# q, k and v as seven-for-eight block products, and linear attention by token tiles

## The chip, the cores and the metric

The kernel runs on one core of one Trainium2 chip. The time is device microseconds of that core for one execution of the whole program; of several executions the median is given.

## The reference

One decoder layer over 1024 tokens of 1024 features: a gated linear attention (GLA) mixer and a squared-ReLU MLP, each behind an RMS norm and with a residual, then a last RMS norm.

```python
h = rms_norm(x, norm_mix)
q, k, v, r, gk_low = split(h @ w_in, [512, 1024, 2048, 3072])      # 4 heads, 128 for q and k, 256 for v and r
log_a = log_sigmoid(gk_low @ w_gk_up + b_gk) / 16                  # one decay for each token and feature of k
# for each head, in chunks: b = cumsum(log_a) inside the chunk
o     = (q * exp(b)) @ state + causal(sum_c q_c k_c exp(b_i - b_j)) @ v
state = state * exp(b_last) + (k * exp(b_last - b)).T @ v
x = x + (rms_norm(o, g_onorm) * silu(r)) @ w_out
x = x + square(relu(rms_norm(x, norm_ffn) @ w_ff1)) @ w_ff2
out = rms_norm(x, final_norm)
```

All in float32. w_ff1 is 1024 x 4096.

## The kernel before

**Products.** `mm3` makes one product of 128 rows by 128 by up to 512 columns as three matmuls: `split` (L84 to L87) cuts each operand into a high part (a rounding copy on ACT, L86) and a low part (the difference, on DVE, L87), and PE adds hi x hi, hi x lo and lo x hi in PSUM. PSUM has eight banks, five of the tag `gl` and three of `mm`.

**The mixer.** A loop over the eight 128-row slices of x (`load_x`) makes q, k and v of head 0. The split x stays in SBUF, in eight tiles `big` (X(half, high or low, slice)), for the whole mixer. Then the heads follow one another. `gate` (L308) makes the decay of a head and half of the tokens: one matmul, Abs, Exp, Ln and Relu on ACT, an add and four scans on DVE. `prep_fast` (L329) scales q and k by the exponentials, `scores_fast` makes the scores of four token tiles as plain fp32 products and splits what the rest needs. `chunk` (L410) does one token tile of one head: new state (three passes of 256 columns), output from scores and v (three passes), output from q and the state (three passes, both split), and the row norm. `chunk_out` (L457) transposes the output into `og`. PE's order is written out by hand: `head_steps` lists the steps of each head, and between them stand pieces of `fill`, the plain projections of q, k, v and r of the later heads (`q_steps`, `v_steps`, `r_steps`, eight slices each, v with 256 columns and q, k, r with 512). DMAs of weights come by `unit` on SP's queue, one tile `raw` of 512 KB each, and are split when they land.

**Block products.** From L597 on, w_out and the MLP are done with 2 x 2 blocks and seven products for eight (`form`, `Side`, `step`, `plan`): each step is 48 matmuls of 512 columns (four lanes of 128 rows, four slices, three passes), needs a new pair of split operands (four `big` tiles, sums on DVE or POOL first), and the lanes' banks go by a sink to their place. `operand` issues the operands of the next step ahead of the current one; ACT's, DVE's and SP's order is set by the scheduler from that.

Of the kernel before, what the change touches and what calls it, by code (L numbers as in the profile page):

```python
# [48 lines left out]
def hybrid_trunk(ctx: ExitStack, tc: tile.TileContext, x, xT, w_head, w_r, w_gk, w_up,  # L49
# [6 lines left out]
    BUFS = dict(big=8, raw=2, w8=3, v8=2, qk=5, og=8, L=2, t4=3, at=1, t2=1, c4=2,  # L56
                S=1, Shl=1, on=2, wup=1, st=8, mm=3, gl=5)
    SHAPE = dict(big=[P, 4, 512], raw=[P, 1024], w8=[P, 2, 1024], v8=[P, 2, 1024], qk=[P, 1024],
                 og=[P, 1024], L=[P, 2, 512], t4=[P, 2, 512], at=[P, 512], t2=[P, 2, 512],
                 c4=[P, 1024], S=[P, DV], Shl=[P, 2, DV], on=[P, DV], wup=[P, 512], st=[P, 8],  # L60
                 mm=[P, 512], gl=[P, 512])
    count = [0]

    def new(tag, dtype=F32):
        count[0] += 1
        pool_ = ps if tag in ("mm", "gl") else sb
        return pool_.tile(SHAPE[tag], dtype, tag=tag, bufs=BUFS[tag], name=f"{tag}{count[0]}")

    def f32(ap):
        return ap.bitcast(F32)  # L70

    def flat(ap):
        return ap.rearrange("p a b -> p (a b)")
# [49 lines left out]
    dma = {}  # L123

    def unit(src, tag="w8"):

        raw = new("raw")
        hl = [new(tag, F32R), new(tag, F32R)] if tag == "c4" else new(tag, F32R)
        hi, lo = hl if tag == "c4" else (hl[:, 0, :], hl[:, 1, :])
        with tc.high_priority():  # L130
            dma["unit"] = nc.sync.dma_start(raw, src)
            split(hi, lo, raw)
        return hi, lo

    def run(general):
        stat = {n: sb.tile([P, w], F32, tag=n, bufs=1, name=f"{n}{int(general)}")
                for n, w in dict(ss1=8, rstd1=8, ss2=8, rstd2=8, rstd3=8).items()}
        ss1, rstd1, ss2, rstd2, rstd3 = (stat[n] for n in ("ss1", "rstd1", "ss2", "rstd2", "rstd3"))

        xs = [[[new("big", F32R) for kh in range(2)] for hl in range(2)] for hf in range(2)]

        def X(hf, hl, kt):
            return xs[hf][hl][kt // 4][:, kt % 4, :]

        def xtok(t, hl, kt):
            return X(t // 4, hl, kt)[:, (t % 4) * P:(t % 4) * P + P]

        xraw = {}  # L150

        def scaled_x(kt, hf, raw):
            r, g = raw[:, hf * 512:(hf + 1) * 512], g_mix[:, kt:kt + 1]
            dve.tensor_scalar(X(hf, 0, kt), r, g, None, op0=ALU.mult)
            dve.scalar_tensor_tensor(X(hf, 1, kt), r, g, f32(X(hf, 0, kt)), op0=ALU.mult, op1=ALU.subtract)  # L155

        def load_x(kt):
            raw = new("og")
            order_after(tc, nc.sync.dma_start(raw, xT[kt * P:(kt + 1) * P, :]), dma["unit"], wait=False)
            for hf in range(2):  # L160
                scaled_x(kt, hf, raw)

        def first():

            xr, wr = new("og"), new("raw")
            w = new("w8", F32R)
            hi, lo = w[:, 0, :], w[:, 1, :]
            with tc.high_priority():
                nc.sync.dma_start(xr[:, 0:512], xT[0:P, 0:512])
                nc.sync.dma_start(wr[:, 0:512], w_head[0, 0][:, 0:512])  # L170
                nc.sync.dma_start(xr[:, 512:], xT[0:P, 512:])
                dma["unit"] = nc.sync.dma_start(wr[:, 512:], w_head[0, 0][:, 512:])
                for cs in (slice(0, 256), slice(256, 512)):
                    split(hi[:, cs], lo[:, cs], wr[:, cs])
                scaled_x(0, 0, xr)
                scaled_x(0, 1, xr)
                split(hi[:, 512:], lo[:, 512:], wr[:, 512:])
            return hi, lo

        pq = [new("mm") for _ in range(2)]  # L180
        pk = [new("mm"), new("gl")]
        pv = [new("gl") for _ in range(4)]
        rbc = new("c4")

        def qk_part(kt, w, hf, passes=(0, 1, 2)):
            for o, c0 in ((pq, 0), (pk, P)):
                for n in passes:
                    mm(o[hf], w[n // 2][:, c0:c0 + P], X(hf, n % 2, kt), kt == 0 and n == 0, kt == KT - 1 and n == 2)

        def v_part(kt, w, hf, passes=(0, 1, 2)):  # L190
            for t in range(4 * hf, 4 * hf + 4):
                o = pv[t // 2][:, (t % 2) * DV:(t % 2) * DV + DV]

                for n in passes:
                    mm(o, xtok(t, n % 2, kt), w[n // 2][:, 256:512],
                       kt == 0 and t % 2 == 0 and n == 0, kt == KT - 1 and t % 2 == 1 and n == 2)

        def token_rms():
            for t in range(TT):
                xr = new("og")  # L200
                nc.sync.dma_start(xr, x[t * P:(t + 1) * P, :])
                act.activation(xr, xr, AF.Square, accum_out=ss1[:, t:t + 1])
            rstd_of(rstd1, ss1, 8, D)

        def spread_rms():
            dg = new("t2")
            for hf in range(2):
# [36 lines left out]
        def half(hf):  # L244
            return slice(hf * 512, hf * 512 + 512)
# [741 lines left out]
```

## Time and profile before

| | |
|---|---|
| time, three runs | median 1040.15 us (1038.79 to 1040.63) |
| the profiled execution | 1039.07 us, its span 1037.4 us |
| PE, busy | 1024.9 us |
| DVE, busy | 706.0 us |
| ACT, busy | 535.2 us |
| SBUF and HBM traffic by DMA | 127.65 MB, 123 GB/s in the mean |
| w_out's first product starts | 334.47 us |

The span is cut into 40 equal slices in the page, and the digit of a slice is its busy share in tenths. A row of the order in time reads: start, length, engine, line, operation, written tile <- read tiles, shapes, count. A group reads: line, engine, operation, tiles, shape, count | busy us, mean ns | idle before, and what ended it. As matmuls overlap, the time of one is best read from the start of a row to the start of the next.

### The profile page before, as it was taken

The page shows a single profiled execution, that of the slowest core. Times are in us where ns is not written, and L with a number is a line of the kernel's source. Part 1 is how long each engine was busy: PE and PEld are TensorE (multiplying, and loading weights), DVE is VectorE, ACT ScalarE, POOL GpSimd, SP SyncE. Part 2 cuts the span into 40 slices and gives each one's busy share as a digit, 9 for nine tenths or more (in the row PEclk, how much of TensorE's full clock was granted, in tenths as well). Part 3 has the DMA queues.
Part 4 walks back from the last instruction along what each step waited for, and adds up shares of the span by engine and source line. Part 5 has one row for each costly group of instructions (what it writes and reads, how often), then busy time and mean ns, then how long its engine had stood idle before and what let it go on. Part 6 is the DMA issues. An engine that isn't in the chain of part 4 may idle for free.

```text
span 1037.4 us, 13340 instructions
## 1 busy us (share of the span) xinstructions
PE 1024.9 (99%) x5122; PEld 871.8 (84%) x5122; DVE 706.0 (68%) x976; ACT 535.2 (52%) x922; POOL 187.5 (18%) x135
## 2 busy tenths in 40 slices
PE   8999999999999999999999999999999999999996
PEld 8989999889888888888888888888888888888885
DVE  7565746467657998879977327976337975438975
ACT  2545747467666357766532447332437331547355
POOL 0000101000000000022404430404430304431261
PEclk9999999999999999999999999999999999999998
DMA  8501111111303433575132674043664044662004
GB/s 282 218 26 37 41 41 42 42 31 52 101 2 133 152 87 116 202 265 211 33 103 101 243 284 163 1 122 105 269 234 162 2 121 161 246 233 90 1 1 166
DMA packets 61977, 127.65 MB, mean 123 GB/s; under 512 B 3920, under 2 KB 36816, under 8 KB 54736
## 3 DMA queue, kind: packets, MB, share of 16 engines
q1 hardware_dynamic: 61760, 126.70, 34.6%
q8 instruction: 42, 0.69, 0.3%
q14 instruction: 31, 0.25, 0.1%
q10 hardware_dynamic: 144, 0.01, 0.0%
HBM read 107.82 MB, written 18.87 MB: 122 GB/s over the span
## 4 chain that ended last, share of the span: by engine, by line
PE 97%; DVE 1%; ACT 1%; DMA 1%; issue 1%; SPq 0%; ACTq 0%; DVEq 0%
PE gl L77 51%; PE mm L77 44%; PE mm L775 1%; PE gl L461 1%; DMA og<-in_xT 1%; PE gl L363 0%; ACT st L845 0%; ACT og L850 0%; DVE big L155 0%; DVE st L848 0%; DVE t L729 0%; DVE w L87 0%; ACT st L846 0%; ACT og L844 0%; DVE qk L729 0%
## 5 line engine op out<-in xcount | busy, mean ns | idle before, releaser
L77 PE MATMUL gl<-big,big 128*128 128x512 f32 x2052 | 476.2, 390 | 0.0
L77 PEld LDWEIGHTS gl<-big,big 128*128 128x128 f32 x2052 | 384.7, 188 | 79.2
L77 PE MATMUL mm<-big,big 128*128 128x512 f32 x972 | 228.9, 389 | 0.0
L77 PEld LDWEIGHTS mm<-big,big 128*128 128x128 f32 x972 | 182.5, 188 | 37.8
L87 DVE TENSOR_TENSOR big<-w,big 128x1024 fp32r<-128x1024 f32 x90 | 128.5, 1457 | 98.3 <-ACT big L86 98.3
L77 PE MATMUL mm<-big,w 128*128 128x512 f32 x744 | 180.5, 393 | 1.5 <-ACT w L86 1.0
L77 PEld LDWEIGHTS mm<-big,w 128*128 128x128 f32 x744 | 136.4, 188 | 28.1 <-ACT w L86 1.2
L86 ACT ACTIVATE big<-w 128x1024 fp32r<-128x1024 f32 x90 | 91.3, 1052 | 117.5 <-PE gl L77 55.0
L624 POOL TENSOR_TENSOR w<-w,w 128x1024 f32<-128x1024 f32 x28 | 77.9, 2796 | 159.6 <-DVE big L87 159.3
L624 POOL TENSOR_TENSOR w<-w,v 128x1024 f32<-128x1024 f32 x14 | 33.3, 2398 | 327.7 <-DVE big L87 327.1
L87 DVE TENSOR_TENSOR big<-og,big 128x1024 fp32r<-128x1024 f32 (+1 forms) x52 | 60.7, 1174 | 43.6 <-ACT big L86 43.6
L87 DVE TENSOR_TENSOR big<-v,big 128x1024 fp32r<-128x1024 f32 x36 | 49.0, 1376 | 37.9 <-ACT big L86 37.9
L86 ACT ACTIVATE big<-og 128x1024 fp32r<-128x1024 f32 (+1 forms) x52 | 47.0, 952 | 53.0 <-PE gl L77 32.5
L77 PE MATMUL mm<-w,big 128*128 128x256 f32 x576 | 73.0, 284 | 0.0
L77 PEld LDWEIGHTS mm<-w,big 128*128 128x128 f32 x576 | 70.9, 192 | 0.2
L86 ACT ACTIVATE big<-raw 128x1024 fp32r<-128x1024 f32 (+1 forms) x42 | 38.2, 935 | 61.1 <-DVE raw L624 33.7
L86 ACT ACTIVATE big<-v 128x1024 fp32r<-128x1024 f32 x36 | 36.6, 1048 | 54.4 <-PE mm L77 27.8
L87 DVE TENSOR_TENSOR big<-raw,big 128x1024 fp32r<-128x1024 f32 (+1 forms) x42 | 60.1, 1457 | 2.0 <-ACT big L86 2.0
L624 POOL TENSOR_TENSOR w<-v,w 128x1024 f32<-128x1024 f32 x14 | 41.1, 2945 | 44.7 <-DVE big L87 44.7
L86 ACT ACTIVATE w<-raw 128x1024 fp32r<-128x1024 f32 (+2 forms) x26 | 25.7, 992 | 39.8 <-PE mm L77 27.5
L798 ACT ACTIVATE og<-og 128x1024 f32<-128x1024 f32 x24 | 25.4, 1057 | 30.5 <-DVE og L791 30.5
L87 DVE TENSOR_TENSOR w<-raw,w 128x1024 fp32r<-128x1024 f32 (+2 forms) x26 | 29.6, 1141 | 15.6 <-ACT w L86 15.4
(209 smaller groups left out, 1010.7 us busy)
## 6 DMA issues: line engine op xcount, KB each, us to landing
big<-xv SPq DMA_DIRECT2D x42, 1024.0 KB, 6.9
xv<-big SPq DMA_DIRECT2D x14, 1024.0 KB, 4.9
v<-in_w_ff SPq DMA_DIRECT2D x32, 256.0 KB, 4.2
w<-in_w_ff SPq DMA_DIRECT2D x32, 256.0 KB, 4.3
w<-in_w_ff SPq DMA_DIRECT2D x16, 512.0 KB, 8.5
v<-in_w_ff SPq DMA_DIRECT2D x16, 512.0 KB, 6.6
raw<-in_w_head SPq DMA_DIRECT2D x15, 512.0 KB, 4.2
og<-in_x SPq DMA_DIRECT2D x8, 512.0 KB, 8.8
```

What stands on the lines that cost most here:

```text
L77: pe.matmul(o, w, m, start=start, stop=stop, skip_group_check=partial)
L86: act.activation(hi, src, AF.Copy)
L87: dve.tensor_tensor(lo, src, f32(hi), op=ALU.subtract)
L461: pe.transpose(tp[:, j * P:(j + 1) * P], on[:, j * P:(j + 1) * P], ident)
L624: self.eng.tensor_tensor(*(self.ap(b, kp, self.span) for b in (o, x_, y_)), op=op)
L775: pe.transpose(p_[:, c * P:(c + 1) * P], xn[4 * hf + c][:, kt * P:(kt + 1) * P], ident)
L798: act.activation(d2, d2, AF.Relu)
```

## The change

The block products now also serve the projections of the mixer. Plan (0) makes q and k of all heads at once: the weights of q and k (2 x 2 blocks of 512) are one side, x the other, seven steps. Plan (1) makes v the same way, with x as its stationary side. The x operands of plan (0) are written to DRAM (`keep`, `xv`) and read back for v and for r; those of steps 0 and 5 of plan (1) are made anew (`KeptX`). Plan (0) has three hooks: the first half of the gate's low-rank product after its first step (`gk_first`), the squares of x's rows (`token_rms`) and a split of block 12 (`x12_split`) ahead of its third step, and the second half (`gk_second`) ahead of its sixth. The gate and the scaling of q and k hang in plan (1) as hooks, as do the loads of r's weights and the first scores. The row scale of RMS norm is no longer applied to q, k and r as they leave PSUM but folded into the vectors `r_sq`, `r_qs`, `r_neg` and `r_ss`.

Then a loop goes over the eight token tiles, each step for all heads: new state, output, transposes of the tile before, and between them the four parts of r of the next tile, now with the tokens as the stationary side and 512 columns of w_r. The product of q with the state is one plain fp32 matmul of 256 columns instead of three passes, and its operands aren't split. w_out and the MLP keep their arithmetic; their tiles have other tags.

```diff
-        fill = (q_steps(1) + v_steps(1) + q_steps(2) + v_steps(2) + q_steps(3) + r_steps(0) + v_steps(3)
-                + r_steps(1) + r_steps(2))
...
+            for i, (_, _, _, sink, order) in enumerate(plan):
+                for at, n in enumerate(order):
+                    for f in hooks.get((i, at), ()):
+                        f()
+                    cur = ops.pop(0)
...
+                    if nxt[0] < len(plan):
+                        ops.append(operand(*nxt))
...
+        def qk_into(n, lane, p_):
+            d = qk_view(int(PART[n][0]) - 1, lane)[:, half(int(PART[n][1]) - 1)]
+            with tc.high_priority():
+                if n in (3, 4, 5):
+                    dve.tensor_tensor(d, p_, d, op=ALU.add)
+                else:
+                    act.activation(d, p_, AF.Copy)
...
+        def token_rms():
+            for t in range(TT):
+                xr = new("g4")
+                nc.sync.dma_start(xr, x[t * P:(t + 1) * P, :])
+                act.activation(xr, xr, AF.Square, accum_out=ss1[:, t:t + 1])
...
+            def split(self, n):
+                out = [kl(new("big", F32R)) for _ in range(2)]
+                for kh in range(2):
+                    if n in (0, 5):
+                        raw = new("raw")
...
+                        for k in range(2):
+                            scaled_split(out[kh][:, k, 0, :], out[kh][:, k, 1, :], raw[:, half(k)], kt + k)
+                    else:
+                        nc.sync.dma_start(out[kh].rearrange("p k l t -> p (k l t)").bitcast(F32), xv[n][kh])
...
+        def outputs(c):
...
+            for h in range(H):
+                d = o[h // 2][:, (h % 2) * DV:(h % 2) * DV + DV]
+                mm3(d, *hl_of(ah, h, P), *hl_of(v[c][h // 2], h % 2, DV), True, c == 0)
+                if c:
+                    mm(d, qk_view(0, h)[:, c * P:c * P + P], S[:, h * DV:h * DV + DV], False, True)
...
+        def load_wr(a, kq):
+            raw = new("raw")
+            for k in range(2):
+                nc.sync.dma_start(raw[:, half(k)].rearrange("p (f c) -> p f c", c=P),
+                                  w_r[4 * a:4 * a + 4, :, (2 * kq + k) * P:(2 * kq + k + 1) * P].rearrange("f p c -> p f c"))
+            w = kl(new("big", F32R))
+            split(w[:, :, 0, :], w[:, :, 1, :], raw.rearrange("p (k f) -> p k f", k=2))
+            wr[a, kq] = w
...
+        def r_part(t, n):
...
+            a, i = ((0, 0), (1, 0), (1, 1), (0, 1))[n]
...
+            for k in range(4):
+                kt = 4 * i + k
+                w = wr[a, kt // 2][:, kt % 2]
+                mm3(rbank[a], u[:, 2 * k, :], u[:, 2 * k + 1, :], w[:, 0, :], w[:, 1, :], kt == 0, kt == 7)
...
+        hooks = {(0, 1): (gk_first,), (0, 2): (token_rms, x12_split), (0, 5): (gk_second,)}
+        if not general:
+            hooks.update({(1, 0, 0, 3): (spread_rms,),
+                          (1, 0, 2, 3): (g(prep_fast, 0, 0, "mm"), g(prep_fast, 1, 0, "mm")),
+                          (1, 0, 3, 3): (g(prep_fast, 2, 0, "mm"),),
+                          (1, 1, 0, 1): (g(prep_fast, 3, 0, "mm"),),
+                          (1, 5, 2, 3): (g(prep_fast, 0, 1, "mm"),),
+                          (1, 6): tuple(g(load_wr, 0, kq) for kq in range(4)),
+                          (1, 6, 3, 1): (g(operands, 0, "mm"),)})
+        chunks_of([(wqk, xq, 0, qk_into, PLAIN), (KeptX(), wv, 1, v_into, PLAIN)], ops_a, hooks, {})
...
+        load_xt(0, 0)
+        load_xt(0, 1)
+        for kq in range(4):
+            load_wr(1, kq)
+        v_split(0)
+        for n in range(4):
+            r_part(0, n)
+        for c in range(TT):
...
+            more = c + 1 < TT
+            if more:
+                load_xt(c + 1, 0)
+                load_xt(c + 1, 1)
+                new_state(c)
+                r_part(c + 1, 0)
+            outputs(c)
+            if more:
+                v_split(c + 1)
+                r_part(c + 1, 1)
+                if not general:
+                    if c + 1 < H:
+                        prep_fast(c + 1, 1, "gl")
+                    operands(c + 1)
+                r_part(c + 1, 2)
+            if c:
+                outputs_T(c - 1, "gl")
+            if more:
+                r_part(c + 1, 3)
```

What moves on the engines, at three places. On PE, before: one tile of head 1's attention with the v product of head 2 behind it (on and L are the output and the scaled q or k, og 840 and 841 hold v's two parts, t the split scores, q and k, Shl the state, w the split v weights, big the x).

```order
L461 MATMUL gl_1550<-ident,on_1390 128x128 x2
L77 MATMUL gl_1556<-og_840,t_1433 128x256
L77 MATMUL gl_1556<-og_841,t_1433 128x256
L77 MATMUL gl_1556<-og_840,t_1433 128x256
L77 MATMUL gl_1555<-og_840,t_1431 128x256
L77 MATMUL gl_1555<-og_841,t_1431 128x256
L77 MATMUL gl_1555<-og_840,t_1431 128x256
L77 MATMUL gl_1555<-Shl_1493,t_1432 128x256 x3
L77 MATMUL mm_1583<-w_1513,big_88 128x256 x2
L77 MATMUL mm_1583<-w_1513,big_90 128x256
```

On PE, now: the second token tile (wa holds the split scores and k, wb v and the tokens of r, g_1599 the state in fp32, hq_291 and hq_300 q, big the r weights).

```order
L70 MATMUL gl_1745<-wb_1649,wa_1689 128x256 x6
L70 MATMUL gl_1746<-wb_1650,wa_1689 128x256 x6
L70 MATMUL mm_1769<-big_1391,wb_1739 128x512 x6
L70 MATMUL mm_1769<-big_1397,wb_1739 128x512 x6
L70 MATMUL gl_1784<-wb_1649,wa_1688 128x256 x3
L70 MATMUL gl_1784<-g_1599,hq_291 128x256
...
L70 MATMUL mm_1822<-big_1491,wb_1739 128x512 x6
L70 MATMUL mm_1822<-big_1497,wb_1739 128x512 x6
```

The state's update and the output of one head, three passes each, have become those of four heads in a row, with one fp32 matmul for the state's share, and what stands between is r at 512 columns instead of v at 256.

On ACT, before: the beginning of head 0's attention, where v of head 1 leaves PSUM (L262) and one weight unit is split (L86).

```order
L86 ACTIVATE w_1239<-raw_1238 128x1024
L453 ACTIVATE on_820,st_819<-gl_802 128x256
L442 ACTIVATE Shl_811<-S_809,st_807 128x256
L110 ACTIVATE st_819<-st_819,vec 128x1
L111 ACTIVATE st_819<-st_819 128x1
L455 ACTIVATE on_820<-gl_802,st_819 128x256
L262 ACTIVATE og_840<-mm_842,rstd_84 128x256
```

On ACT, now: from plan (0) to plan (1). The gl banks are those of the last q/k step, big_771 and big_772 x for v's first step (scaled by g_mix), big_787 and big_790 v's weights.

```order
L426 ACTIVATE hq_505<-gl_248 128x512
L426 ACTIVATE hq_505<-gl_252 128x512
L426 ACTIVATE hq_520<-gl_256 128x512
L426 ACTIVATE hq_520<-gl_260 128x512
L324 ACTIVATE big_771<-raw_773,vec 128x512 x2
L324 ACTIVATE big_772<-raw_779,vec 128x512 x2
L79 ACTIVATE big_787<-wa_679 128x2x512
L79 ACTIVATE big_790<-wa_680 128x2x512
L441 ACTIVATE vx_884<-gl_871,tok_88 128x512
```

Where one weight unit of 1024 stood ahead of the products that use it, there are now four evacuations of 512 columns and then the operands of the next step.

On DVE, before: the gate and scaling of head 0 (t_654 is the gate's input, qk_639 the decay, L_664 and L_674 the scaled q and k) with one weight unit between.

```order
L320 TENSOR_TENSOR t_654<-t_654 128x512
L342 TENSOR_TENSOR L_664<-L_664,qk_547 128x512
L324 SCALAR_TENSOR_TENSOR qk_639<-ones,t_654 128x128 x4
L251 SCALAR_TENSOR_TENSOR qk_625<-mm_697,c_104 128x512
L87 TENSOR_TENSOR w_836<-raw_835,w_836 128x1024
L333 TENSOR_TENSOR L_674<-qk_639 128x512
```

On DVE, now: the first steps of v. g_967 and g_1002 are the gates of heads 1 and 2, hq the q and k, vx the v tiles being added up, and big_1024 a weight operand of v's third step.

```order
L502 SCALAR_TENSOR_TENSOR g_967<-ones,g_967 128x128 x4
L516 TENSOR_TENSOR hq_505<-g_947,hq_505 128x512
L511 TENSOR_TENSOR g_967<-g_967 128x512
L515 TENSOR_TENSOR hq_291<-g_947,hq_291 128x512
L439 SCALAR_TENSOR_TENSOR vx_943<-mm_1082,tok_88,vx_943 128x512
L499 TENSOR_TENSOR g_1002<-g_1002 128x512
L516 TENSOR_TENSOR hq_505<-g_967,hq_505 128x512
L502 SCALAR_TENSOR_TENSOR g_1002<-ones,g_1002 128x128
L515 TENSOR_TENSOR hq_291<-g_967,hq_291 128x512
L439 SCALAR_TENSOR_TENSOR vx_998<-mm_1096,tok_88,vx_998 128x512
L502 SCALAR_TENSOR_TENSOR g_1002<-ones,g_1002 128x128 x3
L80 TENSOR_TENSOR big_1024<-wa_867,big_1024 128x2x512
```

Three preparations stand in a row with the accumulations of v, ahead of the operand's low part, where before one head's preparation had the plain products of another head beside it.

More of the change, by code (lines that the diff above doesn't have):

```diff
@@ L157, in load_x, with half @@
[L157 to L161, printed above, removed]
+        r_sq, r_qs, r_neg, r_ss = (stat["tok"][:, 8 * n:8 * n + 8] for n in range(4))
+        e_in, e_out, e_mid = (stat["est"][:, 32 * n:32 * n + 32].rearrange("p (h c) -> p h c", c=TT) for n in range(3))
+        def half(hf):
+            return slice(hf * 512, hf * 512 + 512)
@@ L178, in first @@
[L178 to L196, printed above, removed]
@@ L371, in prep_general @@
+        at_general = {}
+        def prep_general(h, hf):
+            a, _ = gate(h, hf, "gl")
+            qh, kh = (qk_view(n, h)[:, half(hf)] for n in range(2))
+            if (hf, h // 2) not in at_general:
+                at_general[hf, h // 2] = new("wa")
+            at = at_general[hf, h // 2][:, half(h % 2)]
             pool.memset(at, 0.0)
```

939 lines of the change are left out of this document (451 added, 488 removed).

## The prediction

> **What bounds the kernel now.** The page comes first, then the waits of its chain, then the stretches and the order in time of the places that the change touches.
>
> ```profile
> PE 1024.9 (99%) x5122; PEld 871.8 (84%) x5122; DVE 706.0 (68%) x976; ACT 535.2 (52%) x922; POOL 187.5 (18%) x135
> ...
> PE   8999999999999999999999999999999999999996
> ...
> PEclk9999999999999999999999999999999999999998
> ...
> PE 97%; DVE 1%; ACT 1%; DMA 1%; issue 1%; SPq 0%; ACTq 0%; DVEq 0%
> ```
>
> PE works from the first slice to the last at full clock, and 97% of the chain that ends last is its own work. So a matmul taken away is time gained, one for one, as long as PE finds its operands; and every moment that PE stands is time lost. Both counts are needed.
>
> ```profile
> 350.00:400.00 50.00, 50.00 (x225) 41.31 (x224) 49.77 (x78) 23.68 (x43) 0.00 (x0) 1.00 0.23 64
> ```
>
> This stretch (PE, weight loads, DVE, ACT, POOL, clock, DMA) belongs to the block products of w_out, which stand in the kernel before. DVE is full for 49.77 of 50 us and yet PE never stands: the block form can be fed, but with nothing to spare on DVE. The change puts the same form where DVE and ACT have other work as well.
>
> ```profile
> 304.28 30.22 PE L77 MATMUL mm<-big,w 128*128 128x512 f32 x132
> 334.33 0.28 PE L77 MATMUL gl<-st,ones 128*128 128x1 f32 x2
> 334.47 10.72 PE L77 MATMUL gl<-big,big 128*128 128x512 f32 x46
> ```
>
> These rows of PE (start, length, count) give the boundary: the mixer's projections and attention end at 334.47, and everything behind it, w_out and the MLP, keeps its arithmetic. From the first row's start to the second's, 30.05 us for 132 matmuls, one of 512 columns takes 0.2277 us.
>
> **PE's own work, part by part.** The 256-column matmuls of before are v and the linear attention:
>
> ```profile
> L77 PE MATMUL mm<-w,big 128*128 128x256 f32 x576 | 73.0, 284 | 0.0
> L77 PE MATMUL gl<-w,big 128*128 128x256 f32 x192 | 25.8, 282 | 0.0
> L77 PE MATMUL gl<-v,t 128*128 128x256 f32 x114 | 17.5, 288 | 0.0
> L77 PE MATMUL gl<-Shl,t 128*128 128x256 f32 x84 | 14.6, 283 | 0.0
> L77 PE MATMUL gl<-og,t 128*128 128x256 f32 x66 | 10.2, 287 | 0.0
> ...
> L77 PE MATMUL mm<-big,w 128*128 128x512 f32 x744 | 180.5, 393 | 1.5 <-ACT w L86 1.0 <-DVE big L155 0.5
> L77 PE MATMUL gl<-big,og 128*128 128x512 f32 x32 | 7.4, 389 | 0.0
> L77 PE MATMUL gl<-big,w 128*128 128x512 f32 x24 | 7.2, 393 | 0.0
> L77 PE MATMUL gl<-c,wup 128*128 128x512 f32 x8 | 3.2, 424 | 0.0
> ```
>
> (Means of single matmuls overlap their neighbours, so I take prices from the order in time.) The first five make 1032 of 256 columns, the last four 808 of 512.
>
> ```profile
> 100.17 3.04 PE L77 MATMUL mm<-w,big 128*128 128x256 f32 x24
> 103.05 0.38 PE L461 MATMUL gl<-ident,on 128*128 128x128 f32 x2
> 103.26 1.06 PE L77 MATMUL gl<-L 128*128 128x128 f32 x8
> 104.16 0.60 PE L363 MATMUL gl<-ident,L 128*128 128x128 f32 x4
> ```
>
> From start to start, 24 of 256 columns take 2.88 us, 0.120 each; four plain fp32 scores (two records each) take 0.90 us, 0.225 each. Removed: 1032 x 0.120 = 123.8 us. In its place the changed kernel has, at 512 columns, 7 steps of 48 for q with k (336), the same for v (336), 384 for r, 32 for the gate's low rank and 8 for its upper half: 1096, that is 288 more, 65.6 us. At 256 columns it has 180 in three passes (96 output, 84 state): 21.6 us. The product with the state becomes one plain fp32 matmul of 256 columns, 28 times, which before doesn't have. Its nearest row is the fp32 score; with twice the columns it is 0.45 us, 12.6 in all. If an instruction cost the same whatever its columns it would be 0.225 (6.3), and if it doubled again 0.9 (25.2). I take 0.45. Sum: 65.6 + 21.6 + 12.6 - 123.8 = **24.0 us less**.
>
> The start stays about as it is: PE's first product began at 5.61 us and now needs an x block and a quarter of w, one split more, against two short waits that went; I count nothing (bounds -1 and +2).
>
> ```profile
> 1.10 3.46 PE L77 MATMUL gl<-ones 128*128 128x128 f32 x16 [1.10 <-DVE ones L94]
> 5.61 0.74 PE L77 MATMUL mm<-big,w 128*128 128x512 f32 x2 [1.04 <-ACT w L86]
> ```
>
> **What PE newly waits for.** A step of 48 matmuls lasts 48 x 0.2277 = 10.9 us. Before, an operand split once served eight tiles or more; now every 10.9 us need four new pairs, and ACT and DVE are queues that run in the order shown above. I followed them at each handover with these prices: 1.0 for an ACT split of 1024, 1.2 for a DVE pass of 1024, 0.6 for an ACT bank evacuation, 0.72 and 0.75 for a scaled split on ACT and DVE, 0.68 for a DVE accumulation, 0.63 for a DVE pass of 512, 0.36 (with the record's overlap taken off) for a scan, 1.05 for a token's square, 0.29 for the gate weight's small split.
>
> ```profile
> 334.50 1.99 ACT L86 ACTIVATE big<-v 128x1024 fp32r<-128x1024 f32 x2
> ...
> 346.76 1.89 DVE L87 TENSOR_TENSOR big<-raw,big 128x512 fp32r<-128x512 f32 x3
> 348.56 2.36 DVE L87 TENSOR_TENSOR big<-w,big 128x1024 fp32r<-128x1024 f32 x2
> 350.83 2.36 DVE L624 TENSOR_TENSOR w<-w,w 128x1024 f32<-128x1024 f32 x2
> ...
> L789 ACT ACTIVATE og<-gl 128x512 f32<-128x512 f32 x36 | 21.3, 592 | 14.6 <-PE gl L77 14.6
> L518 ACT ACTIVATE t<-t,vec 128x512 f32<-128x512 f32 x16 | 11.5, 716 | 0.2
> L155 DVE SCALAR_TENSOR_TENSOR big<-og,vec,big 128x512 fp32r<-128x512 f32 x16 | 11.6, 754 | 0.1
> L729 DVE TENSOR_TENSOR qk<-gl,qk 128x512 f32<-128x512 f32 x40 | 26.6, 681 | 1.9 <-PE gl L77 1.8
> L324 DVE TENSOR_TENSOR_SCAN qk<-ones,t 128x128 f32<-128x128 f32 x32 | 11.4, 406 | 0.0
> L202 ACT ACTIVATE og<-og 128x1024 f32<-128x1024 f32 x8 | 8.4, 1051 | 15.1 <-DMA og<-in_x 13.4 <-issue 1.7
> L86 ACT ACTIVATE og<-og 128x128 fp32r<-128x128 f32 x4 | 1.1, 294 | 0.0
> ...
> w<-in_w_ff SPq DMA_DIRECT2D x32, 256.0 KB, 4.3
> ```
>
> 1. q/k step 1 to 2: ACT meets the first evacuation 2.0 us before the step's end. Behind it stand three more (2.4 in all), two weight splits (2.0), four small ones (1.1), x's block 21 (1.0), four scalings of block 12 (2.8) and the last split (1.0): 10.3 us, then 1.2 on DVE, so the last operand comes 9.5 us behind the step's end, and the gate's weight 3.8 behind it. Twelve of the gate's products (2.7 us) lie in that time: **6.8**.
> 2. Start of the third step: behind the accumulation of the last bank (0.68) DVE has a weight sum (1.2) and then the split that PE needs (1.2): **3.1**.
> 3. Start of the fifth: eight ACT passes of about 1.0, five of them squares of tokens, stand between the evacuations; the split of x's block 22 comes behind the fourth evacuation, at 14.1, plus 1.2 on DVE, where the step before ends at 10.9. It is 4.4, and small passes between make it **5.0**.
> 4. q/k to v: ACT takes the last evacuation (0.6), four scaled halves of x's splits (2.9) and only then the weight's split (1.0): 4.5, then DVE 1.2: **5.7**.
> 5. Third step of v: behind the step's last accumulation (0.68) DVE has three scans (1.1) and then the split (1.2), 3.0 at the least. Three gate preparations with the accumulations, 9 x 0.63 + 12 x 0.36 + 4 x 0.68 = 12.7 us, go ahead of it in the 11 us from the first gate's end on ACT, and two ACT passes of each lie between them, so I put DVE 2.5 behind: **5.5**.
> 6. v to token tiles: r's second half of weights goes through two raw buffers, each filled (4.3) only when ACT (1.0) and DVE (1.2) have emptied it. The big buffers come free at the end of v's last step, which goes lane by lane. Worked through, four units in two rounds make PE stand 5.4 if the two transfers of a unit land together; in a row they would take 8.6 and make it 18. They are issued back to back, so near the first: **7.0**.
>
> Inside a token tile I count none: a tile has 20 us of PE work and ACT and DVE about 14 each; between the transposes that make the next state's operand and their use, PE has 5.5 to 6.1 us of r, against 5.1 that the split needs behind the gate's passes. From the last tile to w_out the buffers are free a tile ahead, and the rows of w_out above show no wait. Sum of the waits: 6.8 + 3.1 + 5.0 + 5.7 + 5.5 + 7.0 = **33.1 us**.
>
> **The sum.** 1039.07 (the profiled execution; its span of 1037.4 and 1.67 around it) - 24.0 + 33.1 = 1048.2. That execution lies 1.1 us below the median of the runs shown, so I forecast 1048, 0.8% above the median of 1040.15. With waits from 25 to 40 us it is 1040 to 1055.
>
> **Rivals.**
>
> The other side: ACT and DVE get a lead. The first two waits (9.9 us) are time in which these engines work on; if the lead lasts, the waits 3, 4 and 5 vanish (16.2 us) and the time is 1048 - 16 = **1032**, faster. It decides whether at the fifth step ACT is ahead by more than 4.4 us. For it speaks the stretch of w_out, where DVE is full and PE never stands. Against it: an evacuation can't start before its step ends, and at q/k to v the splits stand behind one.
>
> The clock falls in the gaps.
>
> ```profile
> 1026.00:1028.00 2.00, 1.58 (x7) 0.96 (x6) 1.21 (x5) 1.58 (x5) 0.00 (x0) 1.00 0.40 141
> 1031.00:1032.00 1.00, 0.00 (x0) 0.00 (x0) 0.34 (x1) 0.37 (x1) 0.00 (x0) 0.75 0.65 252
> 1032.00:1034.00 2.00, 0.00 (x0) 0.00 (x0) 0.00 (x0) 0.00 (x0) 0.00 (x0) 0.50 0.76 276
> ```
>
> PE's last matmul ends near 1027.6, and the clock is 0.75 in the mean from 1031 to 1032, then 0.50: it halves after about 3.9 us without work. The program's first eight fp32 products took 3.46 us, 0.43 each instead of 0.225, so a return costs about 1.7 us. Three waits pass 3.9 us (3, 4 and 5) and the first part of wait 1 with 3.8 is at the point; with all four it is 1048 + 4 x 1.7 = **1055**. Against it: waits 1 and 6 come in pieces, and in the others one early lane may start and break them. [...]
>
> Tokens: if the margin of 0.4 us behind the transposes is not there, each of seven tiles waits, say, 1.5 us (one DVE pass of 1.2 and a part): 1048 + 10.5 = **1058**.
>
> The block form pays in full, with ACT and DVE ahead at all six places: 1039.07 - 24.0 = **1015**. The first handover speaks against it, as x's second block is scaled on ACT behind the evacuations.
>
> **How the numbers follow.** Forecast 0.46, lead 0.22, clock 0.12, tokens 0.12, all hidden 0.08. About 0.2% is what a measurement of this kernel can tell from no change, so "same" is 1038.1 to 1042.2: 0.05 of the forecast (its low end, or the fp32 product at 0.225) and 0.06 of the lead (one of the three waits left). Faster: 0.16 + 0.08 = 0.24; same 0.11; slower 0.41 + 0.12 + 0.12 = 0.65. The range must leave at most 0.2 out: all hidden and a little of both ends, so 1031 to 1062, the upper end being the fp32 product at 0.9 (12.6 more) or two of the slower cases in part. The forecast's own range is 1040 to 1055.
>
> **What would show it.** In the changed profile, PE's idle time should be near 40 us instead of 12, nearly all before w_out, in six pieces: the first three released by ACT and DVE splits into big, the fourth by ACT's scaled split, the fifth by DVE, the sixth by a DMA into raw or the split of it. PE's count should be about 4586, and w_out should start near 343. Prices to look at: the plain fp32 256-column product, and whether the granted clock dips. I am wrong if ACT's queue is ahead at the fifth step, if the token tiles show waits of their own, or if PE stands in w_out or the MLP, where I count nothing.

## The result, and the profile after

The changed kernel takes 1055.4 us (median of 4 runs, 1053.9 to 1055.9) beside 1039.5 us of the kernel before: a ratio of 1.0151, 95% interval 1.0133 to 1.0168. It is 1.5% slower, in the range that was forecast and 7 us above its point. PE is the engine that multiplies matrices and PEld the loading of its weights, DVE the vector engine, ACT the scalar engine, POOL the GpSimd engine, and SP issues the DMAs. The page of the changed kernel, the lines that answer to those shown of before:

```profile
PE 1016.8 (96%) x4614; PEld 842.8 (80%) x4614; DVE 730.7 (69%) x910; ACT 548.2 (52%) x828; POOL 198.5 (19%) x114
...
PE   7889889999999999999999999999999999999996
...
PEclk9999899999999999999999999999999999999998
...
PE 87%; ACT 4%; DVE 4%; DMA 3%; issue 1%; SPq 1%; ACTq 0%; DVEq 0%
```

PE has 508 records fewer and is busy only 8 us less. Of the first six of the 40 slices, 158 us, all but the fourth are below nine tenths, and the fifth shows a lower clock. ACT, DVE and DMA have 11% of the chain that ended last, where they had 3%. PE's order in time, at the places where it waits (start, length, work; in brackets the idle time ahead and who ended it):

```profile
23.30 5.52 PE L70 MATMUL mm<-big,g 128*128 128x512 f32 x16 [4.26 <-DVE g L80]
28.66 1.52 PE L70 MATMUL gl<-big,big 128*128 128x512 f32 x6
...
42.75 1.49 PE L70 MATMUL gl<-big,big 128*128 128x512 f32 x5 [2.83 <-DVE big L80]
44.04 5.83 PE L70 MATMUL mm<-big,big 128*128 128x512 f32 x18
49.71 1.52 PE L70 MATMUL gl<-big,big 128*128 128x512 f32 x6
...
68.22 0.50 PE L70 MATMUL gl<-big,big 128*128 128x512 f32 x1 [2.03 <-ACT big L79]
70.42 1.82 PE L70 MATMUL gl<-big,big 128*128 128x512 f32 x5 [1.70 <-DVE big L80]
...
112.44 0.80 PE L70 MATMUL gl<-big,big 128*128 128x512 f32 x1 [4.08 <-ACT big L79]
113.70 5.06 PE L70 MATMUL gl<-big,big 128*128 128x512 f32 x11 [0.46 <-DVE big L80]
...
145.11 1.46 PE L70 MATMUL gl<-big,big 128*128 128x512 f32 x5 [3.94 <-DVE big L80]
...
205.91 0.50 PE L70 MATMUL mm<-big,wb 128*128 128x512 f32 x1 [0.37 <-ACT big L79]
...
215.41 4.19 PE L70 MATMUL mm<-big,wb 128*128 128x512 f32 x17 [0.51 <-DVE big L80]
```

They stand where they were expected: behind the first q/k step, at the third and the fifth, from q/k to v, at v's third step, and (with four more pieces between the last two rows, 4.15 us in all) at the first token tile. In a row they are 4.3, 2.8, 3.7, 4.5, 3.9 and 4.15 us, 23.4 together. But behind each of the first five PE is slow, too: the 16 products from 23.30 to 28.66 take 5.36 us where 16 x 0.2277 is 3.64, and the 23 from 42.75 to 49.71 take 6.96 instead of 5.24. The stretches of the second wait tell why (busy us of PE, PEld, DVE, ACT, POOL, then the granted clock, DMA's share and GB/s):

```profile
40.00:42.75 2.75, 0.00 (x0) 0.00 (x0) 2.72 (x4) 1.09 (x2) 0.00 (x0) 1.00 0.02 6
44.00:46.00 2.00, 2.00 (x6) 1.58 (x5) 1.99 (x3) 1.83 (x4) 0.00 (x0) 0.50 0.97 397
```

The clock halves at 44.0, when PE has been at work again for 1.25 us. By the same count the five waits cost 1.7, 1.7, 1.7, 2.4 and 1.7 us more (9.3). The program's first step loses 1.8 as well: its 48 products, from 6.19 to 19.05, take 12.86 us, where the 48 from 55.15 take 11.04. But no fall is on record there: the first record of the granted clock in the trace is full clock from 9.84 us on (from 4.09 in the kernel before), and ahead of it nine of these products stand in 3.65 us, where at 0.2277 there would be 16. Behind the mixer there is one more place:

```profile
346.41 5.73 PE L70 MATMUL gl<-big,big 128*128 128x512 f32 x24
353.00 0.33 PE L669 MATMUL mm<-ident,g 128*128 128x128 f32 x1 [0.86 <-DVE g L659]
353.99 2.11 PE L669 MATMUL mm<-ident,g 128*128 128x128 f32 x7 [0.66 <-DVE g L659]
355.75 8.13 PE L70 MATMUL gl<-big,big 128*128 128x512 f32 x30
```

The transposes of the last token tile stand in w_out's first step and wait there for its norm: 1.5 us, and about 1.5 at half clock behind it. Together: 24.7 us more of standing, 12.6 us of slow clock. As the span is 16.6 us longer (1054.0 against 1037.4), PE's work at full clock must be 20.7 us less.

### The profile page after: what moved, and what is told of

It reads as the page before. It is cut to its first block, busy times and chain, and to the rows that moved or that the text cites. A ratio compares the mean times of both kernels' runs of the same rounds, so it can differ in the third digit from the quotient of the medians.

```text
span 1054.0 us, 12272 instructions
## 1 busy us (share of the span) xinstructions
PE 1016.8 (96%) x4614; PEld 842.8 (80%) x4614; DVE 730.7 (69%) x910; ACT 548.2 (52%) x828; POOL 198.5 (19%) x114
## 4 chain that ended last, share of the span: by engine, by line
PE 87%; ACT 4%; DVE 4%; DMA 3%; issue 1%; SPq 1%; ACTq 0%; DVEq 0%
PE gl L70 52%; PE mm L70 33%; DMA raw<-in_w_r 1%; DMA wb<-in_w_head 1%; DVE big L80 1%; ACT big L79 1%; PE mm L870 1%; DVE g L502 1%; ACT g L405 1%; ACT big L324 0%; PE gl L669 0%; DMA wa<-in_w_head 0%; DVE vx L835 0%; DVE vx L439 0%; PE gl L589 0%
## 5 line engine op out<-in xcount | busy, mean ns | idle before, releaser
L70 PE MATMUL gl<-big,big 128*128 128x512 f32 x2508 | 590.7, 393 | 16.3 <-DVE big L80 8.9
L70 PEld LDWEIGHTS gl<-big,big 128*128 128x128 f32 x2508 | 473.2, 189 | 117.1 <-DVE big L80 10.8
L80 DVE TENSOR_TENSOR big<-wa,big 128x1024 fp32r<-128x1024 f32 (+1 forms) x112 | 152.3, 1385 | 108.7 <-ACT big L79 108.6
L79 ACT ACTIVATE big<-wa 128x1024 fp32r<-128x1024 f32 (+1 forms) x112 | 112.0, 1037 | 128.2 <-PE gl L70 58.3
L168 POOL TENSOR_TENSOR wa<-wa,wa 128x1024 f32<-128x1024 f32 x28 | 75.2, 2691 | 160.5 <-DVE big L80 159.6
L70 PE MATMUL mm<-big,wb 128*128 128x512 f32 x384 | 96.7, 400 | 4.1 <-DVE big L80 2.2
L80 DVE TENSOR_TENSOR big<-hq,big 128x1024 fp32r<-128x1024 f32 x48 | 61.4, 1282 | 45.9 <-ACT big L79 45.9
L70 PEld LDWEIGHTS mm<-big,wb 128*128 128x128 f32 x384 | 70.3, 188 | 20.5 <-DVE big L80 3.7
L80 DVE TENSOR_TENSOR big<-raw,big 128x1024 fp32r<-128x1024 f32 x50 | 76.7, 1545 | 9.6 <-ACT big L79 9.6
L835 DVE TENSOR_TENSOR vx<-gl,vx 128x512 f32<-128x512 f32 x95 | 63.1, 681 | 6.9 <-PE gl L70 6.7
```

Of the source, the lines that this page charges most:

```text
L70: pe.matmul(o, w, m, start=start, stop=stop, skip_group_check=partial)
L79: act.activation(hi, src, AF.Copy)
L80: dve.tensor_tensor(lo, src, f32(hi), op=ALU.subtract)
L168: self.eng.tensor_tensor(*(self.ap(b, kp, 2) for b in (o, x_, y_)), op=op)
L835: return dve.tensor_tensor(xd, p_, xd, op=ALU.add)
```

## The experiments

Two theories stood against each other. A: each wait is made by what stands ahead of the next operand in ACT's and DVE's order, and most waits are followed by a time at half clock; so moving what stands ahead takes both away. C: the first 200 us are bound by DMA (its share is mostly 0.75 to 1.1 in the first 110 us), and moves in queues help little. For three of the waits the trace of the changed kernel already speaks against C: the DMA engines themselves stand there, with a share of 0.02 from 40.00 to 42.75 (the row above), 0.20 from 66.2 to 68.2 and 0.15 from 108.3 to 112.4. At the first handover it is 1.13 (19.05 to 23.30), at v's third step 0.92 (141.2 to 145.1) and at the first token tile 0.55 in the mean (205.5 to 216) and up to 1.13 in single microseconds; there only runs can decide. For the slow products, B: they have another cause than the pause. Times are medians; the changed kernel's is 1055.4.

**Constant products in the pauses.**

```diff
             pg = new("mm")
+            if hf == 0:
+                keep_warm(pg, 15)
...
+            fills.update({(0, 2): 9, (1, 0): 15, (1, 2): 14})
```

> The changed kernel with 53 idle-time matmuls added: plain fp32 128x128 products of a constant, 15, 9, 15 and 14 of them, ahead of the gate's products, of the third q/k step, of the first and of the third v step, in PSUM banks whose next product overwrites them. They read nothing that those steps wait for, and at 0.225 us each they end before the waited operand comes (gaps of 4.3, 2.8, 4.1 and 3.9 us). Theory A (queues and clock): the gaps themselves stay, but PE is busy in them, the granted clock no longer falls behind them, and each of the four places gains the 1.7 to 2.3 us that 23 matmuls took too long at half clock: about 7 us less than the changed kernel, 1048.5. Rival B (the slow matmuls behind a gap have another cause, such as operand or PSUM traffic): no gain, 1055 or a little more.

Measured: 1051.3 us, ratio to before 1.0122 (1.0105 to 1.0139); 4 us less. PE's order at the third q/k step:

```profile
39.81 2.17 PE L70 MATMUL gl<-ones 128*128 128x128 f32 x18
...
43.02 1.42 PE L70 MATMUL gl<-big,big 128*128 128x512 f32 x5 [0.81 <-DVE big L80]
44.28 4.27 PE L70 MATMUL mm<-big,big 128*128 128x512 f32 x18
```

The operand comes 0.3 us later than before, but the 18 products behind it take 4.27 us instead of 5.83. This place alone doesn't show that the constant products did it: in two of the runs below (the squares later, x first) the same wait of 2.83 us stands unfilled, and the 18 products take 4.25 us there, too. At v's first and third steps it does: in the profiled executions with these waits unfilled (4.1 us in five of them, 3.9 in three) the products behind them were slow each time, 11 in 4.2 to 4.9 us at the first step and 23 in 7.0 at the third, and here they take 2.6 and 5.4. B is out: the same 18 products with the same operands took 5.83 us where the granted clock was 0.50 (44.0 to 46.0), and here 4.27 where it was 1.00. At the first handover there was nothing to win, as the fast products then wait for x's second half (1.0 us at 28.08). So the slow clock there had hidden a late operand, and 4 of the 7 us came.

**The squares of tokens later.**

```diff
-        hooks = {(0, 1): (gk_first,), (0, 2): (token_rms, x12_split), (0, 5): (gk_second,)}
+        hooks = {(0, 1): (gk_first,), (0, 2): (g(squares, 0, 3, "g4"), x12_split), (0, 4): (token_rms,), (0, 5): (gk_second,)}
```

> The changed kernel with the squares of tokens 3 to 7 (and the row scales that need them) moved from the third q/k step to the fifth, in other buffers; nothing is left out. Theory A: the split of x's last block then no longer stands behind five squares in ACT's queue, the wait at the fifth step (2.0 + 1.7 us) goes, and with it the 1.7 us at half clock: 5.4 us less, 1050. Rival C (the first 110 us are bound by DMA, whose share is 0.75 to 1.1 there): the operands come no sooner, under 1 us of change.

Measured: 1053.2 us, ratio 1.0128 (1.0111 to 1.0145). That is less than half of what theory A expected, and none of it was won at this place:

```profile
55.08 0.50 PE L70 MATMUL gl<-big,big 128*128 128x512 f32 x1 [0.78 <-ACT big L79]
58.53 13.90 PE L70 MATMUL gl<-big,big 128*128 128x512 f32 x53 [2.95 <-DVE big L80]
```

The wait at the fifth step is gone (it would stand at 66 to 70), and one of 3.7 us stands at the fourth. With the squares out of the way ACT comes earlier to the split of block 12, its low parts move ahead in DVE's queue, and now these stand before the operand of the fourth step. A wait was moved by one step, not removed: from the end of the third step to the second half of the gate's product both kernels take 27.5 us (55.31 to 82.82 in the changed kernel, 54.30 to 81.79 here). The 2 us come from two places that were not touched and where the clock did not fall in this execution, the third step (18 products in 4.25 us instead of 5.83; 12.6 us from the end of its wait to its own end before, 11.0 now) and w_out (30 products in 7.07 instead of 8.13; 17.3 us from 346.41 to 363.72 before, 16.0 now).

**One gate preparation a step.**

```diff
-                          (1, 0, 2, 3): (g(prep_fast, 0, 0, "mm"), g(prep_fast, 1, 0, "mm")),
-                          (1, 0, 3, 3): (g(prep_fast, 2, 0, "mm"),),
-                          (1, 1, 0, 1): (g(prep_fast, 3, 0, "mm"),),
+                          (1, 0, 2, 3): (g(gate_first, 0), g(gate_first, 1)),
+                          (1, 0, 3, 3): (g(gate_first, 2),),
+                          (1, 1, 0, 1): (g(gate_first, 3),),
+                          (1, 1): (g(prep_later, 0),), (1, 2): (g(prep_later, 1),),
+                          (1, 3): (g(prep_later, 2),), (1, 4): (g(prep_later, 3),),
```

> The changed kernel with the gates' matmuls where they were, but the rest of the four gate preparations (scans, exponentials, scaling of q and k) one for each of v's second to fifth steps instead of three in the second; nothing is left out. Theory A: the weight operand of v's third step is split ahead of the last accumulation, the wait of 3.9 us goes and the 1.7 us at half clock behind it: 5.6 us less, 1049.8. Rival C: v's third step waits for its x operand from DRAM instead; under 1 us of change.

Measured: 1048.6 us, ratio 1.0085 (1.0068 to 1.0101); 6.8 us less. First DVE in the changed kernel, then PE with the gates spread:

```profile
142.24 0.74 DVE L439 SCALAR_TENSOR_TENSOR vx<-mm,tok,vx 128x512 f32<-128x512 f32 x1
142.90 1.04 DVE L502 TENSOR_TENSOR_SCAN g<-ones,g 128x128 f32<-128x128 f32 x3
143.86 1.19 DVE L80 TENSOR_TENSOR big<-wa,big 128x1024 fp32r<-128x1024 f32 x1
```

```profile
132.22 8.32 PE L70 MATMUL mm<-big,big 128*128 128x512 f32 x36
140.38 1.52 PE L70 MATMUL gl<-big,big 128*128 128x512 f32 x6
141.74 4.24 PE L70 MATMUL mm<-big,big 128*128 128x512 f32 x18
```

PE had stopped at 141.2, when DVE was still 1 us of scalings, an accumulation and three scans away from the split. Spread out, v's third step begins without a wait, and its first 18 products in `mm` take 4.24 us where they took 5.88. The gates' matmuls had to stay where they are: the three banks `mm` are taken from v's third step to its fifth.

**Where r's weights land.**

```diff
-            raw = new("raw")
+            raw = new("wa" if a else "raw")
...
-        for n in range(4):
+        for n in (0, 3, 1, 2):
             r_part(0, n)
```

> The changed kernel with r's second half of weights landing in four free weight buffers instead of the two raw ones, and the first tile's r parts in the order 0, 3, 1, 2, so that both that need the first half come first; nothing is left out. Theory A: the six pieces of waiting between 205 and 216 us (4.2 in all) go: the first tile ends up to 5.5 us sooner, at least 2.7 by the order alone; 1050 to 1052.7. Rival C: the weights land no sooner, as the DMA queue's order holds them back, and only the order helps: 2.7.

Measured: 1049.3 us, ratio 1.0096 (1.0079 to 1.0113); 6.1 us less. All of the first tile's r is now one row, 0.24 us a product:

```profile
201.72 11.66 PE L70 MATMUL mm<-big,wb 128*128 128x512 f32 x48
213.22 1.59 PE L70 MATMUL gl<-wb,wa 128*128 128x256 f32 x12
```

What follows it starts at 213.2 instead of 219.4; 0.9 us of this was won before r begins (at 201.7 instead of 202.6), and 5.3 us here. The two buffers had been the cause, as the chain of waits showed it with three transfers into `raw` in a row (4.2, 3.6 and 3.6 us) and the splits of each between them, and not the rate of DMA: its share there was 0.55. Buffers and order were changed together, so how much of the 5.3 each is worth isn't shown; the order alone was expected to bring 2.7.

**x ahead of v's last weights.**

```diff
+                    late = len(plan) == 2 and i == 0
-                    if at == 6:
+                    if at == 6 and not late:
...
+                    if at == 6 and late:
+                        load(i + 1, {True: ("21", "22"), False: ("21",)})
```

> The changed kernel with the loads of v's last two weight blocks queued on SP behind the two x pieces of v's first step instead of ahead of them; nothing else moves in the program, but ACT's queue then has the first scaled splits of x between the last evacuations of q and k. Theory A: the wait at q/k to v (4.1 + 0.5 us) shrinks to about 1.5, the split of the first v weight being behind the third evacuation, and the clock doesn't fall there (2.3 us more): 5 us less than the changed kernel, 1050. Rival C (DMA binds there): x lands as late as before, behind other transfers, under 1 us.

Measured: 1047.7 us, ratio 1.0074 (1.0056 to 1.0092); 7.7 us less. ACT at the handover, first of the changed kernel, then with x first:

```profile
108.40 0.60 ACT L426 ACTIVATE hq<-gl 128x512 f32<-128x512 f32 x1 [0.76 <-PE gl L70]
108.90 2.54 ACT L324 ACTIVATE big<-raw,vec 128x512 fp32r<-128x512 f32 x4
111.35 1.99 ACT L79 ACTIVATE big<-wa 128x1024 fp32r<-128x1024 f32 x2
```

```profile
103.38 0.60 ACT L429 ACTIVATE hq<-gl 128x512 f32<-128x512 f32 x1 [5.84 <-PE gl L70]
103.88 1.33 ACT L327 ACTIVATE big<-raw,vec 128x512 fp32r<-128x512 f32 x2
...
106.67 1.06 ACT L79 ACTIVATE big<-wa 128x1024 fp32r<-128x1024 f32 x1
```

The splits stand between the evacuations, and PE waits 0.4 + 0.8 us instead of 4.5. Some of it comes back a step later (1.9 us at v's second step, where there was none), and at v's third step the wait is 2.4 instead of 3.9 us and the 18 products behind it take 4.25 us, so the clock doesn't fall.

**The clock by itself.**

```diff
+            def gap(n):
+                t, spare = new("gl"), new("on")
+                mm(t[:, 0:P], ones, ones, True, True)
+                act.activation(spare[:, 0:P], t[:, 0:P], AF.Copy)
+                for _ in range(2 * n):
+                    act.activation(spare[:, 0:P], spare[:, 0:P], AF.Copy)
+                t = new("gl")
+                mm(t[:, 0:P], spare[:, 0:P], ones, True, True)
```

> The kernel before the change with eight waits put into the mixer between its plain projections: a small plain fp32 product, then 1, 3, 5, up to 15 copies of 128x128 on ACT one behind the other (about 0.28 us each), then a small product of the result that nothing reads. So PE stands about 0.5, 1.0, 1.6 and so on up to 4.3 us, where it had been busy for 10 us and more on both sides. It measures the clock's rule by itself. Theory A1 (a threshold near 3.9 us, as the end of the program shows): only the longest gap or two are followed by a lower granted clock. Theory A2 (the clock looks at windows that run on their own): the clock falls behind some gaps of 1.5 to 3.9 us too, and not behind others of like length, and each fall costs 1.7 us.

Measured: one execution, 1087.5 us. ACT's other work came between, so the pauses were 0.8, 1.05, 2.17, 2.41, 5.75, 3.92, 7.1 and 7.2 us. PE at the third and the fourth, and the stretches around them:

```profile
172.59 0.49 PE L77 MATMUL gl<-ones,on 128*128 128x128 f32 x2 [2.17 <-ACT on L552]
205.84 0.49 PE L77 MATMUL gl<-ones,on 128*128 128x128 f32 x2 [2.41 <-ACT on L552]
```

```profile
170.08:173.49 3.41, 1.24 (x10) 1.01 (x9) 0.48 (x1) 2.47 (x9) 0.00 (x0) 1.00 0.00 0
173.49:176.90 3.41, 3.41 (x18) 3.41 (x17) 0.95 (x2) 2.36 (x4) 0.00 (x0) 0.50 0.00 0
204.21:207.62 3.41, 1.78 (x9) 1.52 (x10) 0.00 (x0) 1.45 (x5) 0.00 (x0) 1.00 0.00 0
207.62:211.03 3.41, 3.41 (x17) 2.83 (x16) 0.00 (x0) 0.00 (x0) 0.00 (x0) 1.00 0.00 0
```

Behind 2.17 us the clock was at half from 173.5 to 176.9, behind 2.41 us it was not. Behind the four longer pauses it fell each time: behind 5.75 us it was 0.50 from 239 to 245, and behind 3.92, 7.1 and 7.2 the products were slow (48 of 256 columns in 8.4 us instead of 5.8, 24 of 512 in 7.5 instead of 5.5, 120 of 512 in 29.4 instead of 27.3). So it wasn't a threshold on the length of the pause near 3.9 us (A1): short pauses met the fall or missed it (A2). The first two stretches are cut where this trace's clock changes, at 173.49 and 176.90, the others at whole steps of 3.41 us from there.

**All moves together.** Besides those above: the scaling and the split of x's block 12 later, the weight sums behind x's split, the last tile's transposes one lane later, 15 constant products at the first handover.

```diff
-        hooks[0, 0, 1, 3] = (g(outputs_T, TT - 1, "mm"),)
+        hooks[0, 0, 2, 3] = (g(outputs_T, TT - 1, "mm"),)
...
+        plain_form[2] = ("t", (("t", "22", SUB, "t"),))
+        plain_form[3] = ("22", (("12", "22", SUB, "12"),))
```

> The changed kernel with all the moves together, nothing left out: the later squares of tokens, the gates spread over v's steps, r's second half of weights in other buffers and the first tile's order, x ahead of v's last weights, the transposes of the last tile one lane later in w_out; and besides, the scaling of x's blocks 12 and 22 and the split of block 12 queued later, the weight sums of q/k and v behind x's split, and 15 constant products ahead of the gate's to keep the clock up. Theory A (the matmuls saved are a gain of about 22 us, given back by the waits and the clock): 1055.4 less 1.7 (first handover) less 4.5 (third step) less 5.4 (fifth) less 5 (q/k to v) less 5.6 (v's third step) less 5.5 (first tile) less 3.6 (w_out) is 1024; with half of them coming back at the next operand, as the run with the later squares showed, 1032. Both are faster than the kernel before. Rival C (ACT and DVE have no room at all in these 200 us): the waits come back wherever they can, over 1040.

Measured: 1034.0 us, ratio to before 0.9948 (0.9928 to 0.9967): 0.5% faster than the kernel before, and 21 us less than the changed kernel. The largest two groups of what PE still waits for (sum in us, number, longest):

```profile
PE gl L70 <- ACT big L79: 6.1, 4, 4.1
PE gl L70 <- DVE big L80: 4.8, 5, 1.7
```

Of these, 4.8 us stand at q/k to v: here the loads of the moved squares go ahead of x on SP's queue, and x's splits are behind the last evacuation again (this is read from the order of the queues; no run tests it). The rest is 0.2 to 1.7 us a place. C is out: the room on ACT and DVE was there.

**Two more fills.**

```diff
+                          15 if len(plan) == 2 and (i, at) == (1, 0) and not general else 0)
...
-            for _ in range(8):
+            for _ in range(11):
                 mm(warm
```

> The kernel with all the moves, and in two more places constant products where PE stands: 15 ahead of v's first step, where the run with all the moves still waited 4.1 + 0.8 us, and 11 instead of 8 ahead of the program's first product, which so far began at half clock and took 1.75 us more than 48 matmuls need. The waits themselves stay. Theory A: the clock stays up at both, 2 us less at v's first step and up to 1.7 less at the start: 1030 to 1032. Rival B (the slow matmuls don't come from the pause): 1034 as before, or later by the products added.

Measured: 1035.2 us, ratio 0.9959 (0.9945 to 0.9972), no better than without them. The profiled execution was the longest of the five (1039.5); in it the first step did get faster (11.46 us instead of 12.71), but of this 1.1 us only 0.65 was left at the second step (its operand came at 22.77 instead of 23.42) and nothing at the third (39.12 instead of 38.85), and at v's first step the fill didn't hold the clock (0.79 in the mean from 104 to 112):

```profile
101.24 3.51 PE L70 MATMUL gl<-ones 128*128 128x128 f32 x30
105.47 0.50 PE L70 MATMUL gl<-big,big 128*128 128x512 f32 x1 [0.73 <-ACT big L79]
106.73 4.34 PE L70 MATMUL gl<-big,big 128*128 128x512 f32 x11 [0.76 <-DVE big L80]
```

Eleven products in 4.1 us (4.34 less the overlap of the last) instead of 2.5, behind two pauses of under 0.8. In the first run with constant products the same fill stood ahead of the same two pauses, and there the eleven took 2.6 us and the clock did not fall (1.00 from 108 to 116). Filling pauses is no sure cure; the cure is the operand in time.

## Why the prediction was right, and where its sizes were off

- **The six places** were read from the order of the queues, and all six are there, each with the engine that was named. Four runs (the squares later, the gates spread, the other buffers, x first) each took away what stood ahead at one place, and the wait left that place or shrank. The first two places were moved only in the run with all the moves, where 0.9 and 0.4 us are left of them. Their sizes: 6.8 forecast and 4.3 measured, 3.1 and 2.8, 5.0 and 3.7, 5.7 and 4.5, 5.5 and 3.9, 7.0 and 4.15. The sum of the waits was 33.1 and is 23.4. At the first handover, what was counted as a late x operand was covered by slow products (the run with constant products shows it with 1.0 us). At the token tiles, the time is under the lower bound given, 5.4: a transfer into `raw` landed in 2.8 to 4.2 us there (median 3.3), where 4.3 was the price. By the prediction's own terms PE's idle time would have been 12.5 + 33.1 = 45.6 us and not "near 40"; it was 37.2. w_out began at 346.4, where 343 was forecast.
- **The clock** was a rival with 0.12 and a price of 1.7 us a fall, and the time of that rival, 1055, is what came. The price was right (1.7 four times, 2.4 once). The condition wasn't: "three waits pass 3.9 us" counted falls only for long pauses, while the clock fell behind all five, two of them 2.8 and 2.0 + 1.7, and in the run with pauses behind 2.17 us. This is the term that was mis-sized: 0 in the forecast, 12.6 us in the trace, with the start and w_out. The profiled execution (1055.8) lies 7.6 us above the sum of 1048.2: 12.6 for the clock, 3.3 for less work saved and 1.5 for the wait in w_out, less 9.7 for the waits that were over-sized. That the time is near the forecast, and that it meets the rival's 1055, is in part luck: errors of opposite sign. And the 12.6 belong to this one execution: in the profiled executions of two of the runs named above (the squares later, x first) the third step's wait stood at 2.83 us as well, and the 18 products behind it took 4.25 us, not 5.83. Differences of 1.7 us between single executions can be chance.
- **PE's work** was to fall by 24.0 and fell by 20.7. One plain fp32 product of 256 columns is not 0.45 us but 0.38: in the rows below, 12 of 0.120 and 4 of them take 2.95 us (239.03 to 241.98). That gives 2 us back. Against it, changes between kinds of products cost time that no price had: twelve of r behind them take 2.95 us instead of 2.73, and a whole tile (244.93 to 262.99) 18.06 where the prices say 17.6, over seven tiles some 3 us. About 2 us more stay open. The count of 4586 took each of the 28 new fp32 products as one record; with two records each it is 4614, as in the page.

```profile
239.03 0.52 PE L70 MATMUL gl<-wb,wa 128*128 128x256 f32 x3
239.38 0.60 PE L70 MATMUL gl<-g,hq 128*128 128x256 f32 x2
...
241.98 3.12 PE L70 MATMUL mm<-big,wb 128*128 128x512 f32 x12
244.93 0.39 PE L70 MATMUL gl<-g,wup 128*128 128x512 f32 x1
...
262.99 0.39 PE L70 MATMUL gl<-g,wup 128*128 128x512 f32 x1
```

- **The token tiles** were right: from 219 to 346 PE doesn't wait once. **w_out** was wrong: "from the last tile to w_out" looked at the buffers and not at the transposes that stand in its first step (1.5 us, and as much at half clock).
- **The lead** didn't come: after two waits ACT was no further ahead at the fifth step, where it ran evacuations and squares without a pause. That all would be hidden (1015) needs every wait and fall gone; the run with all the moves shows how far away that still is: its 1034 less 10.3 of waits, 3.4 of constant products, 2 at half clock and 1.7 at the start would be about 1016.6.

## What to carry to other kernels

When a change takes work from the engine that bounds and gives the others a new operand for every step, read the queues of the others at each handover before counting the gain: the first operand behind an evacuation is late by everything that stands between. Price a pause with what the clock takes behind it: here a fall cost about 1.7 us, in all about half as much as the pauses. And look where a wait goes when its cause is moved; one step further it may stand again.

## What the runs showed of the hardware

- The clock fell behind pauses of 2.17 us (the run with pauses) and 2.83 us (the changed kernel) and once behind 0.86 + 0.66 us (w_out of the changed kernel), and not behind others of 2.41 (the run with pauses) and, in the runs with the later squares and with x first, again 2.83. It then stayed at half for 3.41 us (173.49 to 176.90) or for 6.83 (112.24 to 119.06), and once it fell when PE had been at work for 1.2 us (at 43.97, with the pause over at 42.75).
- In the changed kernel's trace the changes of the granted clock on record (9.84, 23.49, 26.90, 43.97, 47.38 and so on to 1047.49) lie whole steps of 3.413 us apart, to within 3 ns, and the two of the kernel before (4.09 and 1031.50) 301 such steps. The same wait of 2.83 us, in stretches of that length, in the changed kernel and then in the run with the later squares:

```profile
40.56:43.97 3.41, 1.22 (x5) 1.05 (x6) 3.37 (x4) 2.31 (x4) 0.00 (x0) 1.00 0.18 74
```

```profile
38.14:41.56 3.42, 2.39 (x11) 1.65 (x9) 3.12 (x5) 1.42 (x2) 0.00 (x0) 1.00 0.56 217
41.56:44.97 3.41, 1.62 (x7) 1.36 (x8) 3.32 (x5) 2.25 (x4) 0.00 (x0) 1.00 0.29 120
```

In the first, 2.19 us of the wait lie in one stretch, PE is busy for 36% of it, and the clock falls at its end; in the second the wait is cut into 1.04 and 1.79, the stretches are 70% and 47% busy, and the clock is 1.00 in both. Ahead of the changed kernel's seven falls (at 23.49, 43.97, 71.28, 112.24, 146.37, 354.58 and 1047.49) PE was busy for 0.18, 1.22, 1.36, 0.00, 1.26, 1.83 and 0.16 of the 3.41 us; no fall came behind 1.63, 1.74 and 1.88 (at 142.96, 67.86 and 214.64). The clock came back behind stretches with 3.36 to 3.41 us of work, and at 115.65 it stayed at half behind 2.75. So near half of a stretch the share alone doesn't tell in this trace whether the clock falls. Less whole steps, the changes lie at 3.01 us behind the start of the span in the changed kernel, at 0.68 in the kernel before and at 2.82 in the run with pauses. The shares rest on the ends of matmuls as the profile models them, and no run was made to test whether the clock goes by them.
